# The blocks of a feed-forward product redrawn, and stored partial rows added in DRAM and by VectorE instead of on the way back into SBUF

## The chip, the cores and the metric

The kernel runs on one core of a Trainium2 chip. TensorE (PE) multiplies, VectorE (DVE) and ScalarE (ACT) work on tiles in SBUF and PSUM, GpSimd (POOL) and SyncE (SP) issue DMAs. The metric is the device time of one execution in microseconds (us); the time shown for a kernel is the median of its runs.

## The reference

One layer of a diffusion backbone over 512 latent tokens of width 1024, with 256 context tokens ahead of them. The token mixer (a pooling branch and a bidirectional mLSTM) comes first; the change lies in the feed-forward part behind it:

```python
x = x + g1 * mix_lat
x = x + g2 * _swiglu(_modulate(x, norm_ffn[l], sh2, sc2), w_ffn_in[l], w_ffn_out[l])
...
return _rmsnorm(x, norm_final)

def _swiglu(h, w_in, w_out):
    g, u = jnp.split(h @ w_in, 2, axis=-1)
    return (jax.nn.silu(g) * u) @ w_out
```

The hidden width is 2816, that is 22 tiles of 128. All values are float32.

## The kernel before

Everything is kept transposed: features on the 128 partitions, the 512 tokens along the free dimension. A float32 operand is split into a rounded high part (a cast by ScalarE, `wh`, `oh`, `gh`) and the remainder (a subtraction by VectorE, `wl`, `ol`, `gl`), and each product is made of three TensorE matmuls: high by high, high by low, low by high (`mm3`). So every weight tile that is loaded costs one cast and one subtraction before TensorE can use it.

**First product.** For each hidden tile `j` the gate and the up product form a 2 by 2 block matrix (gate and up by the two halves of the tokens and of the 1024 input features), and a `Pair` computes it with seven block products instead of eight (Strassen and Winograd's scheme). `prepare` loads the pair's two weight rows, one into `wr` and one into `ur` (512 KB each, by SP), forms the sums S1 to S4 of their blocks on VectorE, and splits all of them. For blocks named in `sent` the low part is made by a DMA that adds the weight from DRAM onto the negated high part (`ol`, issued by POOL, L1036). `front` runs the products A11, S1, S2 and A12, `back` runs S3, S4 and A22. After S3, VectorE adds bank and copy (`third`, L1124); A22 is added onto the same bank, so TensorE waits for that addition. `done` splits the finished hidden tile into `act`.

**Second product.** The 22 hidden tiles are worked off in blocks, each block multiplied with its part of `w_ffn_out` and added onto the residual:

- a *plain first block* (hidden tiles 0 to 3 before the change): for each of the 8 output rows one sum over the block's tiles with 512 tokens per matmul (`ffn_out`), which VectorE scales by `g2` and adds onto the residual `x1` in SBUF (L1415). Each finished row is stored to a DRAM buffer `x1d`;
- *two blocks of six tiles* (4 to 9 and 10 to 15): the block's hidden tiles are kept as block operands and their sums (`Even`, `Odd`), and four `Out` items compute two output rows each with seven block products. Their results, scaled by `g2`, go to two DRAM buffers `od` (8 rows each, 256 KB a row) by DMAs on POOL;
- a *plain last block* (16 to 21): `x1` is loaded back from `x1d`, both `od` buffers are added onto it by DMAs that accumulate into SBUF (L1477, 16 of them on POOL), and `ffn_out` runs over the two token halves separately, since the final norm of the first half is computed beside the products of the second.

`run` walks over a list of items and interleaves the back of one item with the front of the next; `made(after)` issues the next item's whole preparation one item ahead, and `also(it)` is called after each item and holds the loads of `x1`. Where TensorE passes from the last `Odd` of a block to the first `Out` (`joint`), the whole back of the `Odd` comes ahead of two steps of the item after.

Instructions of one engine are put in order by a scheduler, as far as `issue_after` and data dependencies leave it free; SP and POOL issue their DMAs in that order and stop at the first one whose buffer or source is not ready. `wr` has three buffers, `ur` two. PSUM has four `ps` banks and four `pat` banks; the plain sums take three of the `ps` banks in turn. At the very end `dense(8)` and `dense(9)` issue matmuls whose result nobody reads, around the last sums of squares.

## Time and profile before

| | before |
|---|---|
| median of 3 runs | 897.86 us |
| lowest of 3 runs | 897.61 us |
| the profiled execution's own time | 899.67 us |
| its span in the profile | 897.9 us |
| mean granted TensorE clock | 0.993 |
| TensorE matmul busy | 874.6 us, 97% of the span |
| VectorE busy | 652.8 us, 73% |
| ScalarE busy | 470.7 us, 52% |
| GpSimd busy | 98.1 us, 11% |
| mean DMA rate | 150 GB/s |

Times in the profile are counted from the start of the span. "L1124" is a line of the kernel before; in the changed kernel the lines up to about 1130 stand one further down. In a wait, the arrow points at the instruction that ended it. "PEclk" is the granted clock of TensorE, 1.00 being full speed. The feed-forward part that the change touches begins at about 525 us.

### The profile page before, as it was taken

To read this page: it belongs to the slowest core of one execution; us is meant where nothing else is said; L and a number is where in the kernel's file an instruction comes from. 1 tells how busy PE (TensorE), PEld (TensorE's weight loads), DVE (VectorE), ACT (ScalarE), POOL (GpSimd) and SP (SyncE) were. 2 spreads that over 40 slices of the span, in tenths; PEclk is the share of its full clock that TensorE was granted. 3 is DMA by queue.
4 is the path that set the end of the run, shared out by engine and by line. 5 is a ranking of instruction groups with operands and counts; after the bars stand their busy time and mean duration, and the time that the engine had idled before them with its cause. 6 is when DMAs were issued, how large, how long until landed. Compare 5 with 4: busy or idle time off the path is not lost.

```text
span 897.9 us, 15849 instructions
## 1 busy us (share of the span) xinstructions
PE 874.6 (97%) x6112; PEld 805.4 (90%) x6112; DVE 652.8 (73%) x1292; ACT 470.7 (52%) x919; POOL 98.1 (11%) x137
## 2 busy tenths in 40 slices
PE   9999999999999999999999999999999999998896
PEld 8689798899889998889988899879999999998896
DVE  4678677768876788667886659578888788856544
ACT  4454453545445453354545456446757775755442
POOL 0000000110000100001000000031202220221510
PEclk9999999999999999999999999999999999998999
DMA  9863021445352642526354710379637863794862
GB/s 350 317 201 99 25 71 60 164 129 153 106 177 66 194 112 76 191 69 199 98 153 154 276 48 25 94 211 239 142 103 218 218 147 99 223 283 103 181 127 95
DMA packets 48557, 134.59 MB, mean 150 GB/s; under 512 B 5440, under 2 KB 9824, under 8 KB 47456
## 3 DMA queue, kind: packets, MB, share of 16 engines
q1 hardware_dynamic: 38208, 112.06, 39.0%
q0 software_dynamic: 10272, 21.50, 11.7%
q8 instruction: 48, 0.79, 0.3%
q14 instruction: 29, 0.24, 0.1%
HBM read 123.56 MB, written 9.98 MB: 149 GB/s over the span
## 4 chain that ended last, share of the span: by engine, by line
PE 85%; DVE 6%; DMA 3%; ACT 3%; issue 2%; DVEq 0%; SPq 0%; ACTq 0%
PE ps L188 10%; PE ps L189 10%; PE ps L190 10%; PE ps L198 8%; PE ps L195 8%; PE ps L196 8%; PE pat L348 3%; PE ps L579 3%; PE ps L580 3%; PE ps L581 3%; PE pat L189 2%; PE pat L188 2%; PE pat L190 2%; PE pat L793 2%; PE pat L795 2%
## 5 line engine op out<-in xcount | busy, mean ns | idle before, releaser
L195 PE MATMUL ps<-a,wh 128*128 128x512 f32 x272 | 106.5, 392 | 0.0
L196 PE MATMUL ps<-a,wh 128*128 128x512 f32 x272 | 106.3, 391 | 0.0
L158 ACT CAST wh<-wr 128x1024 fp32r<-128x1024 f32 (+3 forms) x69 | 66.7, 969 | 63.4 <-PE ps L196 34.8
L159 DVE TENSOR_TENSOR wl<-wr,wh 128x1024 fp32r<-128x1024 f32 (+3 forms) x69 | 78.2, 1133 | 28.7 <-ACT wh L158 17.5
L198 PE MATMUL ps<-a,wl 128*128 128x512 f32 x272 | 68.0, 391 | 0.0
L196 PEld LDWEIGHTS ps<-a,wh 128*128 128x128 f32 x272 | 51.1, 188 | 10.2
L198 PEld LDWEIGHTS ps<-a,wl 128*128 128x128 f32 x272 | 50.9, 188 | 10.4
L195 PEld LDWEIGHTS ps<-a,wh 128*128 128x128 f32 x272 | 51.1, 188 | 10.1
L188 PE MATMUL ps<-hp,oh 128*128 128x256 f32 x176 | 50.8, 289 | 8.7 <-DVE tmp L1124 8.1
L1036 POOL DMA_DIRECT2D ol<-in_wffi x42 | 37.1, 882 | 146.6 <-ACT ol L1035 61.5
L188 PE MATMUL ps<-hp,gh 128*128 128x256 f32 x176 | 49.8, 283 | 2.9 <-ACT pat L1086 2.9
L190 PE MATMUL ps<-hp,ol 128*128 128x256 f32 x176 | 50.3, 286 | 0.0
L189 PE MATMUL ps<-hp,oh 128*128 128x256 f32 x176 | 50.2, 285 | 0.0
L189 PE MATMUL ps<-hp,gh 128*128 128x256 f32 x176 | 49.0, 278 | 0.0
L190 PE MATMUL ps<-hp,gl 128*128 128x256 f32 x176 | 48.9, 278 | 0.0
L177 ACT CAST gh<-sg 128x1024 fp32r<-128x1024 f32 (+1 forms) x27 | 26.7, 989 | 41.5 <-DVE sg L1050 26.5
L538 DVE SCALAR_TENSOR_TENSOR pb<-pb,crow_s 128x1024 f32<-128x1024 f32 x32 | 39.1, 1239 | 11.9 <-DMA pb<-in_wada_b 11.8
L188 PEld LDWEIGHTS ps<-hp,oh 128*128 128x128 f32 x176 | 34.6, 197 | 9.4 <-DVE tmp L1124 8.5
L793 PE MATMUL pat<-vh,Sp 128*128 128x258 f32 x144 | 41.1, 285 | 0.0
L794 PE MATMUL pat<-vl,Sp 128*128 128x258 f32 x144 | 40.7, 283 | 0.0
L795 PE MATMUL pat<-vh,Sp 128*128 128x258 f32 x144 | 40.7, 282 | 0.0
L178 DVE TENSOR_TENSOR gl<-sg,gh 128x1024 fp32r<-128x1024 f32 (+1 forms) x27 | 30.9, 1145 | 11.6 <-ACT gh L177 11.6
(422 smaller groups left out, 3031.2 us busy)
## 6 DMA issues: line engine op xcount, KB each, us to landing
wr<-in_w SPq DMA_DIRECT2D x42, 512.0 KB, 3.6
pb<-in_wada_b SPq DMA_DIRECT2D x32, 512.0 KB, 4.3
wr<-in_wffi SPq DMA_DIRECT2D x25, 512.0 KB, 4.8
ol<-in_wffi POOLq DMA_DIRECT2D x42, 256.0 KB, 5.8
ur<-in_wffi SPq DMA_DIRECT2D x19, 512.0 KB, 4.2
ada<-in_wada_a SPq DMA_DIRECT2D x8, 1024.0 KB, 9.9
wr<-in_wffo SPq DMA_DIRECT2D x16, 384.0 KB, 5.2
wr<-in_wout SPq DMA_DIRECT2D x8, 512.0 KB, 3.7
```

The source lines that it names most:

```text
L158: nc.scalar.copy(wh, raw[:, :n])
L159: V.tensor_sub(wl, raw[:, :n], wh.bitcast(F32))
L188: nc.tensor.matmul(dst, wh, ah, start=first and i == 0, stop=False, skip_group_check=on)
L189: nc.tensor.matmul(dst, wh, al, start=False, stop=False, skip_group_check=on)
L190: nc.tensor.matmul(dst, wl, ah, start=False, stop=last and i == n - 1, skip_group_check=on)
L195: nc.tensor.matmul(dst, wh, ah, start=first and i == 0, stop=False)
L196: nc.tensor.matmul(dst, wh, al, start=False, stop=False)
L198: nc.tensor.matmul(dst, wl, ah, start=False, stop=last and i == len(wparts) - 1)
L538: V.scalar_tensor_tensor(wa[:, :D], wa[:, :D], 0.5, crow_s, ALU.mult, ALU.mult, accum_out=mods[:, i:i + 1])
L793: nc.tensor.matmul(o, sh_, vh[:, s, :], start=n == 0, stop=False)
L794: nc.tensor.matmul(o, sh_, vl[:, s, :], start=False, stop=False)
L795: nc.tensor.matmul(o, sl_, vh[:, s, :], start=False, stop=n == len(srcs) - 1)
```

## The change

The blocks are redrawn: the plain first block takes hidden tiles 0 to 4 (five instead of four), the two blocks of seven products take 5 to 10 and 11 to 16, the plain last block takes 17 to 21 (five instead of six). The number of pairs stays 22 and the number of `Out` items stays 8.

- The first block now runs its two pairs (tiles 3 and 4) through `run`, and then the eight output rows; before, three of the output rows were interleaved with the back of the one pair.
- The first six rows of `x1` are stored by POOL as before, the last two by SP, after the preparation of the first item of the second block.
- The first `od` buffer is added onto `x1d` in DRAM, one row per pair, by DMAs on POOL: during the six pairs of the second block of six and two of the last pairs. Each is ordered after the second `ol` DMA of the following item.
- The rows of `x1` are loaded back after the last pair's `ur` load instead of two per pair during the last pairs. In `prepare`, `loaded` now names the `ur` load.
- The second `od` buffer is loaded into SBUF by SP (six buffers for the eight rows) and added by eight VectorE additions, ordered after the last hidden tile's split.
- At `joint` the three steps of the `Odd`'s back now alternate with the steps of the `Out`'s front.

```diff
-        nc.sync.dma_start(b, wb)
-        p["loaded"] = nc.sync.dma_start(a, wa)
+        p["loaded"] = nc.sync.dma_start(b, wb)
+        nc.sync.dma_start(a, wa)
...
-            split(self.s, *self.dst)
+            nc.scalar.copy(self.dst[0], self.s)
+            self.over = V.tensor_sub(self.dst[1], self.s, self.dst[0].bitcast(F32))
...
             joint = isinstance(it, Out) and not isinstance(prev, Out)
+            if joint:
+                next(b)
             if not it.begun:
                 next(f)
+                if joint:
+                    next(b)
                 next(f)
             if joint:
-                for _ in b:
-                    pass
+                next(b)
...
-    od = {c0: dram.tile([KT, P, T], F32, name=f"od{c0}") for c0 in (4, 10)}
+    od = {c0: dram.tile([KT, P, T], F32, name=f"od{c0}") for c0 in (5, 11)}
...
+    starts = (5, 11)
+    turn = itertools.count(NP + 1)
+    plain = [third] + [Pair(j, next(turn)) for j in range(NP + 1, starts[0])]
+    for _ in run(plain).back():
         pass
-    b = third.back()
-    next(b)
-    next(b)
-    wf, af = [], [ffn_bank(), ffn_bank(), banks[3]]
-    for j, acc in enumerate(af):
-        if j == 2:
-            next(b)
-        wf.append(wchunk(j, 0, c1, raw=None if j else tl("ur", [P, D], F32, 2)))
-        mm3_low_last(acc, wf[j][:NP], act[:NP], last=False)
-    for j, acc in enumerate(af):
-        mm3(acc, wf[j][NP:], act[NP:c1], first=False)
-        ffn_out(j, ALL, None, 0, c1, acc)
-        nc.gpsimd.dma_start(x1d[j], x1[j])
-    for j in range(3, KT):
+    turn_[0] = plain[-1].turn % 3
+    c1 = starts[0]
+    for j in range(KT):
         ffn_out(j, ALL, wchunk(j, 0, c1), 0, c1)
-        nc.gpsimd.dma_start(x1d[j], x1[j])
+        if j < KT - 2:
+            nc.gpsimd.dma_start(x1d[j], x1[j])
...
+    for j in (KT - 2, KT - 1):
+        nc.sync.dma_start(x1d[j], x1[j])
...
+    rows = iter([(c, j) for c in starts[:-1] for j in range(KT)])
...
+            bufs["act"] = 2 * (c1 - c0)
             x1[:] = [S("x1") for _ in range(KT)]
-        elif it in plain:
-            with tc.issue_after(plain[min(plain.index(it) + 1, len(plain) - 1)].p["loaded"].ins):
-                for j in itertools.islice(back_, 2):
+        if it in ins[6:] + plain[1:-1]:
+            after = items[items.index(it) + 1].p.get("added")
+            with tc.issue_after(after.ins) if after else ExitStack():
+                for c, j in itertools.islice(rows, 1):
+                    nc.gpsimd.dma_start(x1d[j], od[c][j], accum_op=ALU.add, max_dma_last_dim=2048)
+        if it is plain[-2]:
+            with tc.issue_after(plain[-1].p["loaded"].ins):
+                for j in range(KT):
                     nc.sync.dma_start(x1[j], x1d[j])
-        if it is plain[-2]:
-            with tc.issue_after(plain[-1].p["added"].ins):
-                for j in range(KT):
-                    for c in (4, 10):
-                        nc.gpsimd.dma_start(x1[j], od[c][j], accum_op=ALU.add)
...
+    def added(j):
+        o = tl("od", [P, T], F32, 6, LINE)
+        with tc.issue_after(plain[-1].p["loaded"].ins):
+            nc.sync.dma_start(o, od[starts[-1]][j])
+        with tc.issue_after(plain[-1].over.ins):
+            V.tensor_add(x1[j], x1[j], o)
+
+    for j in range(KT):
+        added(j)
```

How the change moves instructions is seen at two places.

The first is SP's queue of loads at the beginning of the plain last block. `wr` and `ur` are the two weight rows of a pair, `x_1491` and following are the rows of `x1`. Before:

```order
L1018 DMA ur_9137<-in_wffi 128x1024
L1019 DMA wr_9400<-in_wffi 128x1024
L1018 DMA ur_9269<-in_wffi 128x1024
L1472 DMA x_1491_9128<-x1d 128x512
...
L1472 DMA x_1496_9133<-x1d 128x512
L1019 DMA wr_9532<-in_wffi 128x1024
L1472 DMA x_1497_9134<-x1d 128x512
L1472 DMA x_1498_9135<-x1d 128x512
L1018 DMA ur_9401<-in_wffi 128x1024
```

After, where `wr_9558` and `ur_9559` belong to the very last pair, and `od_9838` is the first row of the second `od` buffer on its way to SBUF:

```order
L1020 DMA wr_9558<-in_wffi 128x1024
L1019 DMA ur_9428<-in_wffi 128x1024
L156 DMA wr_9869<-in_wffo 128x640
L1019 DMA ur_9559<-in_wffi 128x1024
L1479 DMA x_1509_9288<-x1d 128x512
...
L1479 DMA x_1515_9294<-x1d 128x512
L1487 DMA od_9838<-od_5503 128x512
...
L1487 DMA od_9853<-od_5503 128x512
L156 DMA wr_9875<-in_wffo 128x640
L156 DMA wr_9881<-in_wffo 128x640
L1479 DMA x_1516_9295<-x1d 128x512
```

Before, two more pairs' `ur` loads stand behind the rows of `x1` in the queue; after, every pair's loads stand ahead of them, and seven rows of `x1` and six of `od` follow in one piece. The last row of `x1` comes two weight loads later, and the last two rows of `od` (not shown) at the end, once two of the six `od` buffers have been read.

The second place is VectorE right behind the last hidden tile's split (`act`), up to the first sums of the plain last block. Before:

```order
L1129 SCALAR_TENSOR_TENSOR tmp_9761<-tmp_9705,tmp_9761 128x256
L1133 SCALAR_TENSOR_TENSOR tmp_9761<-ps_6276,tmp_9761 128x256
L178 TENSOR_TENSOR act_9779<-tmp_9761,act_9778 128x512
L1415 SCALAR_TENSOR_TENSOR x_1491_9128<-ps_6274,lb,x_1491_9128 128x256
L1415 SCALAR_TENSOR_TENSOR x_1492_9129<-ps_6275,lb,x_1492_9129 128x256
```

After, with the eight additions of the rows of `od`:

```order
L1134 SCALAR_TENSOR_TENSOR tmp_9777<-ps_6276,tmp_9777 128x256
L1139 TENSOR_TENSOR act_9795<-tmp_9777,act_9794 128x512
L1489 TENSOR_TENSOR x_1509_9288<-x_1509_9288,od_9838 128x512
L1489 TENSOR_TENSOR x_1510_9289<-x_1510_9289,od_9841 128x512
...
L1489 TENSOR_TENSOR x_1516_9295<-x_1516_9295,od_9859 128x512
L1420 SCALAR_TENSOR_TENSOR x_1509_9288<-ps_6274,lb,x_1509_9288 128x256
L1420 SCALAR_TENSOR_TENSOR x_1510_9289<-ps_6275,lb,x_1510_9289 128x256
```

All eight additions stand in one piece between the last split and the first instruction that reads a bank of the plain last block (L1415, now L1420). At the same place TensorE's order has changed: the 17 matmuls of `dense` stand behind the third sum of the last block,

```order
L190 MATMUL ps_6276<-act_9795,gh_9883 128x256
L191 MATMUL ps_6276<-act_9794,gl_9884 128x256
L1508 MATMUL ps_6277<-hp_5497 128x256 x17
L189 MATMUL ps_6274<-act_9355,gh_9889 128x256
L190 MATMUL ps_6274<-act_9356,gh_9889 128x256
```

where `ps_6276` is the third bank and `ps_6274` the first bank in its second use, while before they stood at the kernel's end:

```order
L190 MATMUL ps_6274<-act_9778,wl_9882 128x256
L1497 MATMUL ps_6277<-hp_5497 128x256 x8
L238 MATMUL pat_6280<-ones,tmp_9922 128x2 x2
L1497 MATMUL ps_6277<-hp_5497 128x256
L238 MATMUL pat_6280<-ones,tmp_10257 128x2 x2
L1497 MATMUL ps_6277<-hp_5497 128x256 x8
```

The scheduler, which orders these matmuls freely, has moved all 17 from the end to the place where TensorE needs the first bank back.

More of the change, by code (lines that the diff above doesn't have):

```diff
@@ L58, in layer_kernel @@
     shifted = {"ac"}
+    bufs = dict(BUFS)
     def open_pool(name, tags, side="left"):
@@ L432, in queries @@
         return [conv_part(lat_tile(Q0 + 2 * h + dk), T, 2 * h + dk,
-                          [tl("q", [P, T + NEXT], F32R, BUFS["q"], LINE)[:, NEXT:] for _ in range(2)]) for dk in range(2)]
+                          [tl("q", [P, T + NEXT], F32R, bufs["q"], LINE)[:, NEXT:] for _ in range(2)]) for dk in range(2)]
     def keys(h):
@@ L1422, in wchunk @@
         return wload(wffo[j][:, c0 * P:c1 * P], (c1 - c0) * P, dst, skip, raw)[0]
[L1427 to L1451 removed]
+    starts = (5, 11)
+    turn = itertools.count(NP + 1)
+    plain = [third] + [Pair(j, next(turn)) for j in range(NP + 1, starts[0])]
+    for _ in run(plain).back():
+        pass
+    turn_[0] = plain[-1].turn % 3
+    c1 = starts[0]
+    for j in range(KT):
+        ffn_out(j, ALL, wchunk(j, 0, c1), 0, c1)
+        if j < KT - 2:
+            nc.gpsimd.dma_start(x1d[j], x1[j])
+    items, ins = [], []
+    for c0 in starts:
         evens = []
@@ L1455, in layer_kernel @@
             evens.append(Even(j, t, j == c0 + 4, evens[0].turn if evens else t))
-            items += [evens[-1], Odd(j + 1, next(turn), evens[-1])]
+            ins += [evens[-1], Odd(j + 1, next(turn), evens[-1])]
+            items += ins[-2:]
         items += [Out(j, next(turn), evens, c0, c0 + 6) for j in range(KT // 2)]
-    c0, c1 = 16, FT
+    c0, c1 = starts[-1] + 6, FT
     plain = [Pair(j, next(turn)) for j in range(c0, c1)]
-    back_ = iter(range(KT))
+    items += plain
+    made(items[0])
+    for j in (KT - 2, KT - 1):
+        nc.sync.dma_start(x1d[j], x1[j])
+    close_pool("late4")
+    close_pool("late0")
+    open_pool("late0", ("bo", "nf", "ev"))
+    rows = iter([(c, j) for c in starts[:-1] for j in range(KT)])
     def also(it):
@@ L1464, in also @@
             close_pool("late0")
-            open_pool("late0", ("act", "before_act", "x1"))
+            open_pool("late0", ("act", "before_act", "x1", "od"))
             tl("before_act", [P, NEXT], F32, 1, LINE)
             shifted.add("act")
+            bufs["act"] = 2 * (c1 - c0)
             x1[:] = [S("x1") for _ in range(KT)]
-        elif it in plain:
-            with tc.issue_after(plain[min(plain.index(it) + 1, len(plain) - 1)].p["loaded"].ins):
-                for j in itertools.islice(back_, 2):
-                    nc.sync.dma_start(x1[j], x1d[j])
-        if it is plain[-2]:
-            with tc.issue_after(plain[-1].p["added"].ins):
-                for j in range(KT):
-                    for c in (4, 10):
-                        nc.gpsimd.dma_start(x1[j], od[c][j], accum_op=ALU.add)
-    made(items[0])
-    for _ in run(items + plain, also=also).back():
-        pass
+        if it in ins[6:] + plain[1:-1]:
[6 more added lines that the diff above has]
+                for j in range(KT):
+                    nc.sync.dma_start(x1[j], x1d[j])
+    for _ in run(items, also=also).back():
+        pass
+    def added(j):
[6 more added lines that the diff above has]
+        added(j)
     SumSq.banks = banks[4:]
```

10 lines of the change are left out of this document (1 added, 9 removed).

## The prediction

> **What bounds the kernel now.** I read the page first: which engine is full.
>
> ```profile
> PE 874.6 (97%) x6112; PEld 805.4 (90%) x6112; DVE 652.8 (73%) x1292; ACT 470.7 (52%) x919; POOL 98.1 (11%) x137
> ```
>
> TensorE is busy for all but about 23 us, so an edit that takes no matmul away can only win back idle time, and the slow clock behind it. The second view is TensorE's waits, over the feed-forward part from 560 us on (total, times, longest).
>
> ```profile
> PE ps L188 <- DVE tmp L1124: 8.1, 2, 4.8
> PE ps L188 <- ACT pat L1086: 2.9, 4, 1.6
> PE ps L188 <- ACT bo L177: 1.2, 2, 0.6
> PE ps L188 <- ACT act L177: 1.2, 1, 1.2
> ```
>
> The first line is more than half of it: two waits, 4.8 and 3.3 us long. In the view by windows I looked for them and for what the clock did; the columns are length, busy time and starts of PE, of weight loads, DVE, ACT and POOL, then the granted clock, DMA share and GB/s.
>
> ```profile
> 604.00:608.00 4.00, 2.69 (x24) 2.49 (x22) 3.74 (x5) 3.05 (x5) 1.03 (x2) 1.00 1.06 271
> ...
> 808.00:812.00 4.00, 0.00 (x0) 0.00 (x0) 1.70 (x4) 0.23 (x1) 0.00 (x0) 0.69 0.35 100
> 812.00:816.00 4.00, 3.92 (x18) 3.93 (x19) 3.51 (x6) 3.87 (x7) 0.62 (x1) 0.50 0.00 0
> ...
> 848.00:852.00 4.00, 1.41 (x6) 1.41 (x7) 3.09 (x7) 3.38 (x7) 3.55 (x4) 0.81 1.12 234
> 852.00:856.00 4.00, 4.00 (x30) 4.00 (x29) 2.15 (x4) 0.62 (x1) 0.81 (x1) 0.77 1.11 232
> ...
> 870.00:880.00 10.00, 10.00 (x90) 10.00 (x89) 4.67 (x11) 4.10 (x10) 0.00 (x0) 1.00 0.01 2
> ```
>
> The last row gives the normal pace of a 128x256 matmul: 10.00/90 = 0.111 us. Behind the first gap the clock is 0.50 and 18 matmuls start where 36 would fit: 18 x 0.111 = 2.0 us more. Behind the second, 36 starts take 5.4 us instead of 4.0: 1.4 us more. So gap A costs 4.8 + 2.0 = 6.8 us, gap B 3.3 + 1.4 = 4.7 us. The chain of waits says what each waited for (start, length, what).
>
> ```profile
> 799.35 10.83 DMA ur<-in_wffi
> 810.27 0.70 DVE sg L1049
> 811.61 0.43 DVE tmp L1124
> ...
> 842.21 6.03 DMA wr<-in_wffo
> 848.26 0.63 ACT oh L171
> 848.91 0.69 DVE ol L172
> 849.60 0.45 DVE act L178
> 850.12 0.43 DVE tmp L1124
> ```
>
> In both, VectorE stood at the first instruction on a weight row that had not landed, and L1124, which TensorE needed, was queued behind it. Who held the two loads up stands in the rows of the lines that load and accumulate `x1`, each with its DMAs' time to landing (minimum, median, maximum), and of `ur`:
>
> ```profile
> L1472 SPq DMA_DIRECT2D x<-x1d x8: 381/416/797, 790.8 to 796.1; - x8
> DMA to landing us min/median/max: 4.7/8.8/12.2
> ...
> L1018 SPq DMA_DIRECT2D ur<-in_wffi x18: 327/328/333, 572.2 to 815.1; - x18
> DMA to landing us min/median/max: 3.0/4.0/10.8
> ...
> L1477 POOL DMA_DIRECT2D x<-od x16: 873/1060/2296, 836.3 to 861.5; - x16
> DMA to landing us min/median/max: 4.7/6.8/11.7
> ```
>
> A: eight rows of `x1` (2 MB) were issued from 790.8 to 796.1, just ahead of the `ur` load of 799.35, which took 10.83 us where the median is 4.0. B: the 16 accumulating DMAs ran from 836.3 to 861.5, over the weight load of 842.21.
>
> **The change part by part.** *Gap A.* No row of `x1` now stands ahead of a pair's load; only single accumulating DMAs fall there. At 4.0 us the load lands 6.8 us earlier, which covers the wait of 4.8. I take off all of A, -6.8 (ends -5.0 if 1.8 of it returns, and -6.8). Late next is the `x1` and `od` traffic behind the last `ur` load, which only the last block's weights share.
>
> *Gap B.* The 16 accumulations are gone from this place; the order of the steps is not: weight split, load, cast, split, `act`, L1124. What stays open is how fast the load lands.
>
> ```profile
> wr<-in_wffo SPq DMA_DIRECT2D x3, 384.0 KB, 4.4
> ...
> wr<-in_wffo SPq DMA_DIRECT2D x5, 256.0 KB, 3.4
> ```
>
> These are the medians of such loads from 817 to 836 and from 565 to 600. The load is now 320 KB, between the two: 3.9 us, 2.1 less than 6.03. Of 3.3 us of idle 1.2 stay; a second small split (128 columns) now comes ahead of `act`, 0.2 more. 1.4 us of idle stay, and I expect the clock to hold, since the window from 604 to 608, with 1.3 us of idle, shows it at 1.00. B: -4.7 + 1.4 = -3.3 (ends -4.7, and 0 if the load still takes 6.03).
>
> *The eight additions.* VectorE does them between the last split and the first L1415. Rows for the pace of such an operation, and for the end of the last pair before:
>
> ```profile
> 817.00 0.69 DVE L1057 TENSOR_TENSOR sg<-sg,wr 128x512 f32<-128x512 f32 x1
> 817.60 0.69 DVE L178 TENSOR_TENSOR act<-tmp,act 128x512 fp32r<-128x512 f32 x1
> ...
> 853.56 0.42 DVE L1133 SCALAR_TENSOR_TENSOR tmp<-ps,tmp 128x256 f32<-128x256 f32 x1 [0.52 <-PE ps L190]
> 854.67 0.69 DVE L178 TENSOR_TENSOR act<-tmp,act 128x512 fp32r<-128x512 f32 x1 [0.69 <-ACT act L177]
> 857.54 0.88 DVE L1415 SCALAR_TENSOR_TENSOR x<-ps,lb,x 128x256 f32<-128x256 f32 x2 [2.17 <-PE ps L190]
> ```
>
> One starts 0.60 us after the other. On the times of before: TensorE ends the pair at 853.5. It then has 24 matmuls on four finished tiles (2.7), 6 on the fifth (0.7) and the third sum of 15 (1.7), and at 858.6 needs the first bank again. VectorE ends the last split at 855.4, the additions at 855.4 + 8 x 0.60 = 860.2, and half of the row of two L1415 (0.88) frees the bank at 860.6. The seventh row of `od` can only be asked for once the first addition has freed its buffer, at 856.0; with 3.4 us (the 256 KB weight load above) it lands at 859.4 where VectorE would want it at 859.0: 0.4 more. So TensorE gets the bank at 861.0, 2.4 us late. The 17 `dense` matmuls (17 x 0.111 = 1.9 us) lie in that wait; 0.5 us stays idle, and the clock should hold. Term: +2.4. Ends: +1.9, what `dense` alone takes there, and +8.8, if the last `od` rows land after the median 8.8 us of the crowded `x1` loads (the eighth, asked for at 856.6, at 865.4; addition 0.6 and L1415 0.44 to 866.4, plus 1.0 of slow clock, half of A's share).
>
> *The end of the kernel.* One `dense` matmul stood between the two last sums of squares:
>
> ```profile
> 888.68 0.22 PE ps L1497
> ```
>
> That goes, -0.2; the runs of eight on either side lay beside ScalarE's square and POOL's power.
>
> *The first block.* The wait for `act` (1.2 us, the last line of the waits) had two matmuls of cover too few per row; now twelve of 512 columns lie ahead of it, so it goes. But the second pair must now be split where VectorE and ScalarE are still at work on the first, and its A11 may wait for its casts. No row shows that; the nearest are the waits for L1086, 0.7 us on average and 1.6 at most. I take 1.2, so 0 in all (ends -1.2 and +2.0). The next pairs' weights get 0.6 us more per output row (15 matmuls instead of 12, at the pace below), which should shorten the L1086 waits at the following transition: -0.5 (ends -1.6 and 0).
>
> *The alternation at the first `Out`.* The two waits for `bo`, the block operands that the `Out` products read, lie there. S3's 12 matmuls (1.3 us) now lie ahead of the first `Out` product: -1.0 (ends -1.2 and 0).
>
> *The tile that moves* from the last block to the first is worked in 24 matmuls of 512 columns instead of 48 of 256.
>
> ```profile
> 592.00:596.00 4.00, 4.00 (x19) 3.31 (x18) 1.35 (x2) 0.62 (x1) 0.54 (x1) 1.00 0.79 256
> ```
>
> A 512-column matmul takes 4.00/19 = 0.21 us: 48 x 0.111 - 24 x 0.21 = 0.3 us, -0.3. The number of seven-product steps is the same.
>
> *The eight accumulations in DRAM.* No row of before shows one. The nearest is the burst into SBUF, whose queue in the window from 838 to 856 read:
>
> ```profile
> q0 software_dynamic: 1558, 2.85, 92.4%
> ```
>
> 2.85 MB, 11 rows of 256 KB, took 92.4% of 16 engines for 18 us: 1.5 us of all engines a row. It is ordered behind the second `ol` DMA of a pair. Gap A shows the slack: 6.8 us late made a wait of 4.8, so 2.0 us are free. 1.5 lies below that. I take +0.8 for the whole (0.1 a row), ends 0 and +12 (8 x 1.5). The Trainium skill, "DMA: Bandwidth & Descriptors", section "Issuing engines are not separate DMA queues", speaks against this part: DMAs issued from ScalarE, SyncE or GpSimd run on the same 16 engines and interleave. Gap A agrees, with 10.83 us against 4.0. By that rule alone, with no slack, this term would be +12 instead of +0.8.
>
> Sum: -6.8 - 3.3 + 2.4 - 0.2 + 0 - 0.5 - 1.0 - 0.3 + 0.8 = -8.9. The profiled execution took 899.67 us (span 897.9), so 890.8 of the same kind; the median of the runs lies 1.8 lower at 897.86, which gives 889.0.
>
> **The rivals.** *Late rows at the end.* The loads of `x1` must wait for the accumulation of their row, and SP stops at the first that cannot go: the seventh and eighth rows' accumulations are issued during the last pairs, and weight loads stand behind both. For: the accumulations into SBUF took up to 11.7 us. Against: they were 16 at once; the minimum is 4.7. Then B keeps its 4.7 and the additions rise by up to 6.4: between 892.3 and 898.7, say 895.5.
>
> *The wait is moved, not removed.* 3.3 MB of `x1` and `od` rows still have to come in within some 30 us, now behind the last `ur` load; the weight row that follows on SP comes late, VectorE stands at its split, and A returns one pair later, with its clock: 889.0 + 6.8 = 895.8. For: the split stands ahead of L1124 in the order. Against: 3.3 MB at the 232 GB/s of the quoted window from 852 to 856 are 14 us.
>
> *Accumulations take the loads' time*: each of the eight costs its pair the 1.5 us, with no slack: 889.0 - 0.8 + 12 = 900.2, within the 2% of no change. Against it: the slack of 2.0 us.
>
> *Slower: the low halves come late.* The `ol` loads share POOL's queue with the accumulations, and one stands right behind each.
>
> ```profile
> 825.36 0.87 POOL L1036 DMA_DIRECT2D ol<-in_wffi  x1 [6.00 <-ACT tmp L1121]
> 828.10 0.87 POOL L1036 DMA_DIRECT2D ol<-in_wffi  x1 [1.87 <-ACT pat L1086]
> ...
> 841.85 0.28 PE L190 MATMUL pat<-hp,ol 128*128 128x256 f32 x1
> ...
> DMA to landing us min/median/max: 3.9/5.8/11.0
> ```
>
> An accumulation would go out at 825.4 + 0.9 = 826.3; the `ol` load issued at 828.1 is needed at 841.85 and takes 5.8 (the last row is L1036's). If it had to wait for the accumulation to land, TensorE stands still from the point at which that takes over 841.85 - 5.8 - 826.3 = 9.8 us. At 13 us, a little over the longest seen, each of the eight costs 3.2 and some 1.4 of slow clock: 8 x 4.6 = 37, giving 925. Against: a single one is nearer to the minimum of 4.7.
>
> *More is won*: the ends on the good side (B whole, first block -1.2, transition -1.6) give about 885.
>
> **How the numbers follow.** Forecast 0.60; late rows 0.14; wait moved 0.10; loads' time 0.06; low halves late 0.04; more won 0.06. The likeliest, 889.0, is the predicted time. From 885 to 896 lie the forecast with its ends, most of "more won", and the first two rivals but for their worst: about 8 in 10; the other two lie above. By over 2% (18 us, about what a measurement of this kernel tells from no change) faster would need nearly all idle time of the kernel gone: 0.02. Slower by over 2%: the low halves late and a little for what I have not seen, 0.05. Within: 0.93.
>
> **What would show it.** In the profile after: no wait for L1124 of over 2 us and a granted clock of 1.00 from 560 us to the last sums; `ur` loads within 6 us; one idle time of TensorE of about half a microsecond behind `dense`, ended by the first L1420; VectorE's eight additions within 5.5 us. Wrong would be: a gap of over 3 us anywhere in the last pairs, additions that wait for `od`, SP held at a row of `x1` while a weight row is due, or matmuls that wait for `ol`.

## The result

The kernel after took 902.27 us (median of 5 runs, 900.06 to 902.96) against 897.61 us for the kernel before beside it. The ratio is 1.0052, with an interval of 1.0031 to 1.0074: 0.5% slower, and not 1% faster as forecast (889.0 us, range 885 to 896). Run twice more, each time beside the kernel before on one chip, it came out at 1.0012 (0.9998 to 1.0026) and 1.0018 (1.0002 to 1.0034). So by the three ratios the loss is between 1 and 5 us, nearer to 1 or 2 in the two larger samples, and the gain is not there. The profiled execution took 900.06 us, the least of its five, with a span of 898.3 us against 897.9 before (899.67 us, above its median), and a mean granted clock of 0.992 against 0.993; so the two profiles show 0.4 us of the difference and account for where the forecast gain went. They do not show why the median lies 2.2 us above the profiled execution. TensorE's busy time, from the page of the kernel after, is what it was (874.6 us before):

```profile
PE 874.0 (97%) x6088; PEld 803.4 (89%) x6088; DVE 657.9 (73%) x1300; ACT 471.5 (52%) x919; POOL 88.7 (10%) x127
```

So the idle time has only changed its place. TensorE's waits of the kernel after from 560 us on (total, times, longest):

```profile
PE ps L189 <- ACT pat L1087: 9.3, 9, 5.7
PE pat L191 <- DMA ol<-in_wffi: 1.4, 1, 1.4
PE ps L191 <- DMA ol<-in_wffi: 1.2, 1, 1.2
PE pat L255 <- POOL rc L247: 1.1, 1, 1.1
...
PE ps L189 <- DVE tmp L1125: 0.4, 1, 0.4
```

The line that led before, 8.1 us in two waits for L1124 (L1125 now), has shrunk to 0.4. In its place stands one wait of 5.7 us for a copy by ScalarE, L1087; TensorE's waits for that copy were 0.7 us on average before. The windows around it (columns as in the prediction) show no matmul for a whole window, and the clock at 0.50 behind it:

```profile
836.00:840.00 4.00, 2.89 (x25) 2.68 (x24) 0.00 (x0) 0.00 (x0) 0.00 (x0) 1.00 0.73 282
840.00:844.00 4.00, 0.00 (x0) 0.00 (x0) 2.72 (x4) 3.58 (x7) 0.67 (x1) 0.81 0.31 77
844.00:848.00 4.00, 3.38 (x16) 3.38 (x17) 1.37 (x3) 1.49 (x4) 0.21 (x1) 0.50 0.46 71
848.00:852.00 4.00, 4.00 (x31) 4.00 (x31) 2.08 (x4) 1.50 (x4) 0.00 (x0) 0.84 0.30 82
```

From 844.6 to 852, 47 matmuls start where 7.4/0.111 = 66 would fit, so some 2 us are lost on top of the 5.7. The chain of waits of the kernel after through that place (start, length, what), and SP's timeline with the instructions that it issued, say why:

```profile
816.86 8.65 DMA x1d<-od
...
825.52 4.48 DMA x<-x1d
...
830.07 9.89 DMA wr<-in_wffo
...
842.89 0.42 DVE tmp L1130
843.31 0.34 DVE tmp L1134
...
844.20 0.37 ACT pat L1087
```

```profile
816.43 9.41 SPq L1479 DMA_DIRECT2D x<-x1d  x7
825.93 2.96 SPq L1487 DMA_DIRECT2D od<-od  x6
829.19 1.22 SPq L156 DMA_DIRECT2D wr<-in_wffo  x2
```

The timelines of ScalarE and VectorE show the split of that load; the brackets give how long the engine had stood idle, and what ended it:

```profile
840.05 0.72 ACT L178 CAST gh<-wr 128x640 fp32r<-128x640 f32 x1 [11.42 <-DMA wr<-in_wffo]
840.80 0.82 DVE L179 TENSOR_TENSOR gl<-wr,gh 128x640 fp32r<-128x640 f32 x1 [9.60 <-ACT gh L178]
```

The third weight row of the last block was asked for at 830.07, behind 13 rows of `x1` and `od` on SP, and took 9.89 us to land; SP itself had stood before the seventh row of `x1` until that row's accumulation landed. ScalarE and VectorE reach the split of that weight row (L178, L179) some 10 us before it can start, and behind that split stand L1130, L1134 and the copy L1087 for which TensorE waits. It is gap A again, with other rows ahead of another load, in a later pair; it is called the new gap below. It is no accident of one execution: in the traces of the two repetitions the wait is 6.2 and 5.6 us long.

The eight additions came as forecast. VectorE's timeline of the kernel after:

```profile
858.86 4.90 DVE L1489 TENSOR_TENSOR x<-x,od 128x512 f32<-128x512 f32 x8
863.68 1.26 DVE L1420 SCALAR_TENSOR_TENSOR x<-ps,lb,x 128x256 f32<-128x256 f32 x3
```

They follow each other without a wait for an `od` row, and TensorE stands still for 0.4 us behind the `dense` matmuls (its wait for L1420).

For the account, the span is cut at instructions that both kernels have: the end of the plain first block's last addition onto `x1`, the second, tenth and sixteenth store of an `Out` result, the end of the last `act`, the first addition onto `x1` with 256 columns. Times in us, from the timelines of VectorE and POOL. "Work moved" is what the table of blocks moves: a pair is 84 matmuls of 256 columns (84 x 0.111 = 9.3), a tile is 24 x 0.21 = 5.0 in the first block and 48 x 0.111 = 5.3 in the last.

| stretch | before | after | work moved | difference left | forecast |
|---|---|---|---|---|---|
| to the end of the first block | 603.3 | 617.9 | +14.3 | +0.3 | 0 |
| to the second store (transition, new turn) | 73.8 | 72.7 | | -1.1 | -1.5 |
| to the tenth store (four `Out`, the six pairs of the second block) | 89.4 | 92.3 | | +2.9 | +0.8 |
| to the sixteenth store (four `Out`) | 24.8 | 25.1 | | +0.3 | |
| last pairs | 64.0 | 50.9 | -9.3 | -3.8 | -10.1 |
| additions | 2.2 | 4.7 | | +2.5 | +2.4 |
| to the end | 40.4 | 34.6 | -5.3 | -0.5 | -0.2 |
| the tile's wider matmuls | | | | -0.3 | -0.3 |
| sum | 897.9 | 898.3 | | +0.4 (+0.3 by the rounded rows) | -8.9 |

Two rows carry the miss: the last pairs, 6.3 us, and the pairs of the second block, 2.1 us. Every other row is within 0.4 us of its forecast.

### The profile page after: what moved, and what is told of

Its sections match the earlier page's. It is cut to its first block, busy times and chain, and to the rows that moved or that the text cites. A ratio compares the mean times of both kernels' runs of the same rounds, so it can differ in the third digit from the quotient of the medians.

```text
span 898.3 us, 15806 instructions
## 1 busy us (share of the span) xinstructions
PE 874.0 (97%) x6088; PEld 803.4 (89%) x6088; DVE 657.9 (73%) x1300; ACT 471.5 (52%) x919; POOL 88.7 (10%) x127
## 4 chain that ended last, share of the span: by engine, by line
PE 72%; issue 8%; DMA 8%; DVE 6%; ACT 4%; POOL 1%; DVEq 0%; POOLq 0%; SPq 0%; ACTq 0%
PE ps L189 8%; PE ps L190 8%; PE ps L199 8%; PE ps L191 8%; PE ps L197 7%; PE ps L196 7%; DMA ur<-in_wffi 3%; PE pat L349 3%; PE ps L580 3%; PE ps L581 3%; PE ps L582 3%; PE pat L794 2%; PE pat L795 2%; PE pat L796 2%; DMA wr<-in_wffo 1%
## 5 line engine op out<-in xcount | busy, mean ns | idle before, releaser
L189 PE MATMUL ps<-hp,gh 128*128 128x256 f32 x176 | 50.9, 289 | 9.4 <-ACT pat L1087 9.3
L189 PE MATMUL ps<-hp,oh 128*128 128x256 f32 x176 | 49.2, 280 | 1.0 <-ACT oh L1032 0.5
L190 PE MATMUL ps<-hp,oh 128*128 128x256 f32 x176 | 48.8, 277 | 0.0
L178 ACT CAST gh<-sg 128x1024 fp32r<-128x1024 f32 (+1 forms) x27 | 26.7, 988 | 39.5 <-DVE sg L1051 30.3
L189 PEld LDWEIGHTS ps<-hp,gh 128*128 128x128 f32 x176 | 33.6, 191 | 11.6 <-ACT pat L1087 11.5
L179 DVE TENSOR_TENSOR gl<-sg,gh 128x1024 fp32r<-128x1024 f32 (+1 forms) x27 | 30.9, 1145 | 11.0 <-ACT gh L178 11.0
```

The lines of the kernel that those rows point to most:

```text
L189: nc.tensor.matmul(dst, wh, ah, start=first and i == 0, stop=False, skip_group_check=on)
L190: nc.tensor.matmul(dst, wh, al, start=False, stop=False, skip_group_check=on)
```

## The experiments

All were run beside the kernel before on one chip; the table has each median, that of the kernel before beside it, and the ratio with its 95% interval. Kernels with the same time of before ran together on one chip; what ran again as a base for its group is in italics. The edits are shown shortened.

| run | us | before | ratio |
|---|---|---|---|
| weight rows first | 898.47 | 899.73 | 0.9988 (0.9976 to 1.0001) |
| dense at the end | 900.61 | 899.73 | 1.0015 (1.0003 to 1.0028) |
| no sums in DRAM | 896.31 | 899.73 | 0.9965 (0.9949 to 0.9981) |
| old turn | 902.33 | 899.73 | 1.0032 (1.0020 to 1.0044) |
| *after, again* | 900.92 | 900.28 | 1.0012 (0.9998 to 1.0026) |
| two rows late | 899.71 | 900.28 | 0.9999 (0.9984 to 1.0014) |
| stores add | 892.49 | 900.28 | 0.9919 (0.9895 to 0.9942) |
| split later | 898.22 | 900.28 | 0.9971 (0.9953 to 0.9989) |
| *stores add, again* | 892.29 | 898.83 | 0.9932 (0.9916 to 0.9948) |
| before, rows late | 892.88 | 898.83 | 0.9927 (0.9909 to 0.9946) |
| first store adds | 898.65 | 898.83 | 1.0000 (0.9987 to 1.0013) |
| before, stores add | 893.01 | 898.83 | 0.9940 (0.9926 to 0.9954) |
| *before, rows late, again* | 892.07 | 898.80 | 0.9913 (0.9889 to 0.9938) |
| after, sums as before | 890.36 | 898.80 | 0.9898 (0.9872 to 0.9923) |
| *after, a third time* | 900.49 | 898.80 | 1.0018 (1.0002 to 1.0034) |
| *after, sums as before, again* | 892.73 | 899.47 | 0.9916 (0.9898 to 0.9935) |
| fifth split later | 890.55 | 899.47 | 0.9895 (0.9876 to 0.9913) |

The theory at the outset: the gain of gap A was taken off, but the wait had moved to the next load that stands behind bulk rows on SP; beside it the accumulations in DRAM cost more than the 0.8 us put down. The rival: the loss lies in the second block and at the end of the kernel alone.

### The weight rows first

```
-    with issue_after(last ur load): load x1[0..7], od rows
+    with issue_after(last ur load): load x1[0..5]
+    weight rows 1, 2, 3 of the last block
+    with issue_after(weight row 3): load x1[6], x1[7], od rows
```

> The kernel after, with one thing moved on SP's queue: the second and third weight rows of the last block are asked for behind the sixth row of x1, ahead of the two rows of x1 that wait for the last accumulations and of the od rows. Theory (the wait was moved, not removed): TensorE's idle time of 5.7 us for L1087 at 838.9 and the 2.0 us of slow clock behind it go, 902.3 - 7.7 = 894.6, and the eight additions still take about 4.9 us in one piece. Rival 1 (it moves once more): the od rows, asked for later, come late to the additions, one to four of which then wait for them; 5 to 7 us come back in front of the first L1420 and the time stays at 900 to 902. Rival 2 (the gap is not where the time went; the accumulations and the end of the kernel are): the gap goes, but under 3 us are won, 899 or more.

Measured 898.47 us: the gap for L1087 is gone, the additions are in one piece, and still only part is won. In its own trace (its lines stand one further down) TensorE's waits and the chain have

```profile
PE ps L190 <- DVE tmp L1126: 5.4, 2, 3.9
```

```profile
836.74 7.27 DMA wr<-in_wffo
844.09 0.73 ACT gh L179
844.85 0.83 DVE gl L180
...
845.70 2.84 DMA wr<-in_wffo
848.56 0.63 ACT oh L173
...
850.62 0.43 DVE tmp L1126
```

The fourth weight row now stands behind the two `x1` rows and the six `od` rows and lands at 844.0. The fifth is asked for when the fourth's split is done (845.70), lands at 848.5, and L1126 stands behind its split: 3.9 us of idle time, and then 1.7 us of slow clock between 852 and 856. The first rival had the right idea (it moves once more) but named the wrong place, the additions. The bulk rows hit whichever weight row comes next.

### Dense at the end

```
-    dense(8); sd = rstd_cols(...); dense(9)
+    with issue_after(last product): dense(8)
+    sd = rstd_cols(...)
+    with issue_after(last sum of squares): dense(9)
```

> The kernel after, with the 17 dense matmuls held behind the last product, eight ahead of the last sums of squares and nine behind them, where the kernel before had them. Theory A (their absence at the end let the clock fall to 0.50 and 0.62 over the last sums and the L255 rows; they covered nothing that matters at the additions): 1.0 to 2.2 us less, 900.1 to 901.3, with a granted clock of 0.9 or more over the last 8 us; TensorE then stands idle for 2.3 us ahead of the first L1420. Theory B (as on record: at the end they lay beside waits and cost or bring nothing; beside the additions they keep the clock up): no change at the end, and the idle time of 2.3 us at the additions brings up to 1 us of slow clock: 902.3 to 903.3.

Measured 1.0015 of before, where the kernel after has 1.0012 to 1.0052: no difference that these runs can tell. The 17 matmuls cover nothing but the idle time that the additions make, as the prediction had it; without them TensorE waits, in this kernel's waits and windows,

```profile
PE ps L190 <- DVE x L1421: 2.4, 1, 2.4
```

```profile
868.00:870.00 2.00, 2.00 (x19) 2.00 (x19) 1.31 (x5) 1.95 (x6) 0.00 (x0) 1.00 0.00 0
```

and the clock stays at 1.00 behind it. At the end of the kernel they are worth 0.5 us at most (34.1 us to the end against 34.6).

### Without the sums in DRAM

```
-        if it in ins[6:] + plain[1:-1]: ... dma_start(x1d[j], od[c][j], accum_op=add)
```

> The kernel after without the eight accumulating DMAs into x1d: the first stored block of six tiles is left out of the sum. Theory A (the accumulations cost far more than the 0.8 us put down for them, in the second block, where the span between the first and the last stored row grew by 4.4 us, and at the end, where the seventh row held SP for 5 us): 3 to 4.5 us come back in the second block and at least 3 us of the 7.7 at the gap for L1087, so 894 to 896. Theory B (0.8 us, and the gap comes from the 3.3 MB themselves, whoever holds SP): 900 to 901.5, with the gap for L1087 still over 4 us. If both hold by half (second block back, gap kept): 898.

This kernel leaves the first stored block out of the sum. Measured 896.31 us, 0.9965 of before, just above theory A's 894 to 896. SP is not held by an accumulation any more, yet most of the new gap stays; this kernel's waits have

```profile
PE ps L189 <- ACT pat L1087: 8.3, 7, 3.7
```

So 2.0 us of the 5.7 came from SP's stand and the accumulations beside it, and 3.7 stay with the rows alone: each theory holds for a part. The six pairs of the second block (eighth to tenth store) took 66.3 us here. Over the kernels, one trace each: with accumulations in DRAM 67.4, 69.2, 67.1 (after, three times), 68.2, 69.2, 67.7, 68.8 and 66.6, mean 68.0; without them, in kernels with the new table of blocks and plain stores, 66.3, 65.4, 65.2 and 65.5, mean 65.6; in the kernel before 64.6. So the accumulations cost 2.4 us there in the mean, with no overlap between the two groups, and up to 1 us comes in with the rest of the change (64.7 and 65.0 in two further traces with the old blocks).

### The old turn into Out

```
-            if joint: next(b)        # back of the pair, in three steps between the fronts
+            if joint: for _ in b: pass
```

> The kernel after with the turn into the first Out of each block as it was: the last step of the pair ahead of it is run to its end behind the first two Out products, not between them. Theory (as on record: the new turn wins 1.0 us, once per block at most): 903.3 to 904.3, with waits for bo of about 1.2 us in all. Rival (the new turn is part of the loss, as TensorE works on the pair's last products while the blocks wait): 900 to 901.5.

Measured 1.0032 of before; the kernel after lies between 1.0012 and 1.0052, so the median settles nothing. The trace has the waits for the block operands back that the prediction spoke of,

```profile
PE ps L189 <- ACT bo L178: 1.2, 2, 0.6
```

and the second block's four `Out` took 26.0 us against 25.1 in all three runs of after. But another kernel with the new turn, the fifth split later, took 26.0 us there too. A gain of up to 1 us from the new turn fits, and is not shown.

### Two rows late

```
-    load x1[0..7] ; od rows ; weight rows 2, 3, 4
+    load x1[0..5] ; od rows ; weight rows 2, 3, 4 ; load x1[6], x1[7]
```

> The kernel after with only the two rows of x1 moved that wait for the last accumulations: on SP's queue they come behind the fourth weight row of the last block; six od rows stay ahead of the second. Theory (what made the weight row late is that SP stood for 5.7 us at the seventh row of x1, and what was then asked for in one bunch): the second and third weight rows land by 833, the fourth by 841, and neither the gap for L1087 (7.7 us with its clock) nor the one for L1126 that came in its place when the od rows were moved too (3.9 us and 1.7 of clock) is there: 902.3 - 7.7 = 894.6, or 0.992 of before. Rival (the twelve rows that still stand ahead are enough to make it late): 3 to 5 us of the gap stay, 898 to 900.

Measured 899.71 us, 1.2 us under after, with a gap of 5.4 us still there. Here the theory failed in one point: not holding SP is not enough. SP's timeline and the chain:

```profile
821.70 8.67 SPq L1488 DMA_DIRECT2D od<-od  x6
830.63 13.17 SPq L157 DMA_DIRECT2D wr<-in_wffo  x3
```

```profile
821.15 10.03 DMA x<-x1d
831.25 10.53 DMA wr<-in_wffo
```

SP did not wait for an accumulation now, but for rows of `x1` to land before it issued the last three `od` rows and the weight rows, the third of which was so asked for at 831.25. Twelve rows are 3.1 MB; at the 251 GB/s that all transfers together moved between 816 and 840 they take 12.5 us, and the weight row behind them lands at 841.8, as late as ever. So no accumulation has to hold SP for the row to be late: the bytes ahead of a load with a date are enough.

### The split later

```
-    wl_ = [wchunk(j) for j in range(8)]
+    wl_ = [wchunk(j) for j in range(2)]
+    with issue_after(third of the last pairs: its act): wl_.append(wchunk(2))
+    wl_ += [wchunk(j) for j in range(3, 8)]
```

> The kernel after with no transfer moved: only the split of the third weight row (cast on ScalarE, subtraction on VectorE) is held until the third of the last five pairs has its act, some eight instructions later on either engine. Theory (the late row costs time because its split stands in order ahead of what TensorE needs): the row lands as late as before, about 840, but the idle time for L1087 falls from 5.7 to about 2.4 us, and the clock holds or falls for less: 902.3 - 3.3 - up to 2.0 = 897 to 899. Rival (TensorE waits for the traffic in another way, through the low halves or its own weights): the idle time stays over 5 us and the time at 901 to 903.

No transfer is moved here, only the order in which ScalarE and VectorE take up the late row. Measured 898.22 us, 2.7 us under after in its group. The waits between 834 and 852 (this kernel's L1091 is L1087, its L1129 is L1125) are

```profile
PE ps L193 <- DVE tmp L1129: 2.2, 1, 2.2
PE ps L193 <- ACT pat L1091: 1.9, 1, 1.9
```

The 5.7 us shrink to 1.9 with the row as late as before, and 2.2 us come back at the fifth row, which is asked for only when the fourth's split is done, with a slow clock from 852 to 856. So the time is lost because the engines take their work in order, and a late operand stops everything queued behind it. The theory held in size and place.

### The kernel before with its rows late

```
-        elif it in plain: (two rows of x1 behind each pair's loads)
+        if it is plain[-2]: with issue_after(last ur load): load x1[0..7]
```

> The kernel before with one thing moved: its eight loads of x1 stand on SP's queue behind the last ur load, not around it. Its 16 accumulating DMAs into x1 stay. Theory (eight rows can be hidden behind the last ur load, sixteen with the weight rows cannot): the gap of 4.8 us and its 2.0 us of slow clock go and do not come back one pair later; the second gap (3.3 + 1.4) stays, as the 16 accumulations still lie over the weight load: 0.992 to 0.993 of before. Rival (a gap is always moved to the next weight row): an idle time of 3 us or more for L1086 or L1124 comes between 830 and 842, and the time is 0.997 to 1.000 of before.

This is the kernel before with one thing moved, and it measured 892.88 and 892.07 us, 6 and 6.7 us under the kernel before. TensorE's waits of its first run, where of the two gaps only a part of gap B is left (2.3 us here, 3.1 in the second run):

```profile
PE ps L188 <- ACT pat L1086: 3.0, 5, 1.6
PE ps L188 <- DVE tmp L1124: 2.3, 1, 2.3
```

Gap A is gone and did not come back one pair later: eight rows (2 MB) behind the last `ur` load make no gap, and twelve or more, in the kernels above, do. The term of -6.8 in the prediction is right for this edit.

### Stores that add

```
-            nc.gpsimd.dma_start(od[c0][2 * j], o)
+            nc.gpsimd.dma_start(x1d[2 * j], o, accum_op=ALU.add)
-    accumulations into x1d, od loads, eight additions
```

> The kernel after with each Out product's store adding its two tiles straight into x1d, for both stored blocks: the 16 stores into od become 16 accumulating stores, and the eight accumulations between DRAM tiles, the eight loads of od and VectorE's eight additions go. Theory: the 2.6 us at the additions, 1.2 to 3.0 us in the second block, and the 7.7 us of the gap go, since SP is no longer held and eight rows less are on the queue: 902.3 - 11.5 to 13.3 = 889 to 891, or 0.986 to 0.988 of before. Rival 1 (an accumulating store moves each byte twice and takes POOL longer, so the low halves behind it on POOL come late): 16 times 0.3 to 0.6 us of that come back, 894 to 900. Rival 2 (the last two stores land late and SP stands at the seventh row of x1 as it did): the gap of 7.7 stays, 897 to 899.

Measured 892.49 us, 8.4 us under after, and 892.29 in a second run. With eight rows only on SP, no idle time over 1.4 us is left in the waits:

```profile
PE ps L189 <- ACT pat L1087: 6.1, 11, 1.4
```

The first rival holds in part. The first of an `Out`'s two stores, accumulating, holds POOL for 0.87 us, not 0.56, and lands in a median of 4.2 us, not 2.4 (the second: 6.4, not 5.2); four `Out` with such stores took 24.8 to 27.0 us, 26.3 in the mean (second to eighth store and tenth to sixteenth, over four runs), against 24.8 in the kernel before and 24.1 to 26.0 in all runs with plain stores.

> The kernel before, with its blocks of 4, 6, 6 and 6 tiles and its own turn into Out, in which each Out store adds straight into x1d, the 16 accumulations into x1 go, and the eight loads of x1 stand behind the last ur load. Theory (the gain lies in the rows that no longer come in over the weight loads, and the rest of the change, five tiles first and last and the new turn, brings the 1.1 us between the first block and the first store and the 0.4 us at the end): both gaps go, and it comes out 1 to 2 us over the kernel of this group whose Out stores add: 0.993 to 0.995 of before. Rival (the rest of the change is a loss, which the stores hide): 2 us or more under it, 0.988 to 0.990.

The same stores in the kernel before, with its rows late, gave 893.01 us, 0.7 us over the kernel of its group with the new blocks. The rival, 2 us or more under it, did not come; the 0.7 us itself is not clear of the noise.

```
+            if first stored block: dma_start(x1d[j], o, accum_op=ALU.add)
+            else: dma_start(od[j], o)
-    accumulations into x1d
```

> The kernel after with the first stored block's Out stores adding into x1d; the second stored block is stored, loaded and added by VectorE as in after. Theory (two costs, one in the second block from the accumulations between DRAM tiles, one at the end from sixteen rows ahead of a weight row): the six pairs of the second block take 65 to 66.5 us, not 67 to 69; the gap for L1087 stays at 3 to 5 us, as where the accumulations were left out; the additions keep their 2.6 us: 5 us under after, 0.995 to 0.997 of before. Rival (only the rows that SP stood at made the gap): the gap falls under 1.5 us, 0.991 to 0.993.

Measured 898.65 us, 1.0000 of before, and the theory missed half: the additions and the gap at L1087 (3.4 us, not under 1.5 as the rival had it) came as expected, but the six pairs took 68.5 us without any accumulation among them. One wait of 2.0 us with a slow clock behind it is in that stretch, in its waits from 734 to 744 and the window behind:

```profile
PE ps L189 <- ACT pat L1087: 2.0, 1, 2.0
```

```profile
742.00:744.00 2.00, 2.00 (x12) 2.00 (x11) 1.72 (x4) 0.00 (x0) 0.54 (x1) 0.54 0.74 195
```

Take off its 2.0 and the 1.7 of clock, and 64.8 is left. Why that wait came here stays open. It also says that the 2.4 us above hold in the mean and not for each trace: two rows late, with its 68.8 us, has such a wait of 2.1 us with a slow clock as well.

### The kernel after with the sums as before

```
-    accumulations into x1d, od loads, eight additions by VectorE
+    for j in range(8): for c in starts:
+        nc.gpsimd.dma_start(x1[j], od[c][j], accum_op=ALU.add)     # during the last pairs, as before
```

> The kernel after (blocks of 5, 6, 6 and 5 tiles, new turn into Out) with the stored rows added as before, by 16 accumulating DMAs into x1 during the last pairs; its eight loads of x1 stand behind the last ur load already. Theory A (the partition and the turn bring what was put down for them, about 1.1 us between the first block and the first store and 0.4 us at the end, and all of the loss is in the new way of adding): 1 to 2 us under the kernel before with its rows moved, 0.991 to 0.992 of before, six pairs of the second block in 64.5 to 66 us. Theory B (part of the loss comes with the partition or the turn: the pairs of the second block stay at 66 us or more without any accumulation there, as where these were left out): 0.5 to 2 us over it, 0.994 to 0.996.

Measured 890.36 us beside 900.49 for after and 892.07 for the kernel before with its rows late; in a second run 892.73. So the new way of adding costs 10.1 us, all of the loss and more, and the new blocks and turn with the old way of adding lie 1.7 us under the old blocks in the one comparison on one chip (the ratios of the four runs, 0.9898 and 0.9916 against 0.9913 and 0.9927, say about 0.13%, with overlapping intervals). Theory A's 1 to 2 us and its six pairs (65.4 and 65.2 us) came, and theory B's loss did not; but whether the new blocks win anything the intervals leave open. What is left is gap B, in a smaller form in this trace (4.2 us in the second run's):

```profile
PE ps L189 <- DVE tmp L1125: 3.2, 1, 3.2
```

> The same kernel with the split of the fifth weight row held on ScalarE behind the fourth of the last five pairs' act cast and on VectorE behind the last pair's L1125 (L1128 in its own numbering); no transfer is moved. Theory (the place of the split in the order): the idle time of 3.2 us and the slow clock of 1.7 us go, and at most 1 us comes back where the next splits follow: 4 to 5 us under the base, 885.5 to 886.5. Rival (the accumulations make the row late for whoever needs it next): the wait turns up at the last pair's act or at the first sums, and under 1.5 us are won.

```
+    held = fourth of the last pairs: its act cast, last pair: its L1125
     wl_.append(wchunk(4))     # cast and subtraction behind these
```

Measured 890.55 us beside 892.73, 0.9895 of before. The wait for L1125 is gone, the clock stays at 1.00, and 0.2 to 1.2 us come back at four places, 2.2 us together; the trace gains 3.4 us of span, the median 2.2, between the theory's 4 to 5 and the rival's 1.5. Both kernels are faster than before and than after: the later rows were worth keeping, the additions were not, and the partition and the turn at least cost nothing.

## Why the prediction was wrong

**What bounds it, and the two gaps:** right. The place, size and cause of both were read rightly; the kernel before with its rows late won 6 to 6.7 us against -6.8 on record.

**The step that failed** is in the paragraph on gap A: "I take off all of A" with "late next is the `x1` and `od` traffic behind the last `ur` load, which only the last block's weights share". What is late next was named and costed at nothing. It was then made a rival ("the wait is moved, not removed") with 0.10, and its description is what happened: VectorE at its split, a weight row late on SP, the clock lost too (the instruction kept waiting was the copy L1087, not L1124). It cost 5.7 + 2.0 us against the 6.8 put down. The argument against it, 14 us of transfer within some 30 us, set the bytes against the whole stretch and not against the first date in it. By the same figures: 13 rows are 3.4 MB, 14.7 us at 232 GB/s; begun at 816.4 they end at 831.1, and the two weight rows of 320 KB behind them at 833.9. In the kernel after TensorE ran dry at 838.9 and went on 4.7 us after the row had landed, so the row was due at 834.2. The sum leaves 0.3 us of slack, where the prediction set 14 us against some 30, and no room for SP's stand or for POOL's transfers, with which the row came at 840.0. A chance of 0.10 was far too low for that; how high it should have been, the rows quoted ahead of the run do not settle, since the date itself comes from the trace after.

The Trainium skill, "DMA: Bandwidth & Descriptors", section "Issuing engines are not separate DMA queues", has DMAs of all issuing engines interleave on the same 16 engines. The trace of the kernel after agrees: POOL's `ol` loads asked for while SP's rows came in (816 to 830) took 6.4 to 8.1 us to land, the one asked for at 843.3 took 4.1. Gap A, which the prediction gives as agreeing, does not test this, since its rows and its late load were both issued by SP.

What the prediction left out is SP's own queue, where the rows stand ahead: in the kernel after, SP's 17 loads from 816.0 to 833.7 landed in the order in which they were asked for, the third weight row (839.97) behind the last of the six `od` rows (838.34).

**Gap B:** 0.4 us of idle time where 1.4 were expected, which was at least in part luck: behind the new gap the row had more time. Where the new gap was taken away or cut while the rows stayed, 2.2 to 3.9 us came back at L1125 (the split later, the weight rows first). The two gaps together, -10.1 on record, measured -3.8.

**The accumulations in DRAM** were mis-sized: +0.8 on record, 2.4 us measured in the second block, and 2.0 of the 5.7 us at SP. The issue on POOL (862, 1186 and 1200 ns) and the landing are in the group of their line:

```profile
L1475 POOL DMA_DIRECT2D x1d<-od x8: 862/1186/1200, 711.7 to 825.8; - x8
...
DMA to landing us min/median/max: 4.4/7.6/8.8
```

The slack of 2.0 us that was to cover them was read from a late load on SP in the last pairs. In the second block POOL stood 3.3 us before the first accumulation until the sixth `od` store had landed (711.20), and the `ol` loads behind the accumulations landed 1.6 to 4.7 us later than in the kernel without them. The +12 that the prediction works out with no slack was further off, on the other side.

**The additions** (+2.4, measured +2.5) and **the end** (-0.2, -0.5) were right; only the 0.4 us for a late `od` row did not come. **The first block** (0, +0.3) was right in the sum and in part by luck: the wait for `act` went as forecast, but of the 1.9 us that came in its place only 0.5 are a wait for a cast (L1032), and 1.4 are the wait for an `ol` load in the list above, which the prediction did not name. **Transition and turn** (-1.5, -1.1): the waits for the copy fell from 2.3 to 1.9 us and that for `bo` from 0.6 to 0.3, and a wait of 0.6 us for the first block's last addition (L1415), at the boundary of the two stretches, is gone, which the prediction did not name. With the old way of adding the new blocks and turn came out 1.7 us better, where -1.8 had been put down for transition, turn and tile; that is not clear of the noise.

**Late rows at the end** was right in that SP stood at the seventh row (5.7 us), wrong in that the additions would wait: they ran in one piece. Three of the four signs of being wrong that the prediction names came: a gap of over 3 us in the last pairs, SP held at a row of `x1`, and matmuls that wait for `ol`. **Accumulations take the loads' time** and **low halves late** did not come at their prices; TensorE's waits for `ol` are 1.2 us in the second block and 1.4 in the first. **The range** was too narrow because two rivals could hold at once: the 6.3 us of the one and the 2.1 us of the other make 8.4 of the 9.3 us between the forecast and the profile, and the range held each alone.

## What to carry to other kernels

Bulk loads that are moved off one load with a date land in front of the next one: for every load behind them ask when its first user stands in line, and set bytes ahead of it against the time up to that date, not against the whole stretch. An engine that works in order stops at the first operand that is late, so a split placed a few instructions later can be worth as much as a load that comes earlier. Of a change with several parts, run each part alone: here the later rows by themselves won 6 to 7 us, and the new way of adding beside them cost 10.

## What the runs showed of the hardware

The clock did not follow the length of a gap alone. It fell to 0.54 behind an idle time of 2.0 us (first store adds, 740 to 742) and to 0.57 behind 2.2 us (the split later), and stayed at 1.00 behind 2.4 us (dense at the end, 865 to 868) and 2.3 us (before, rows late); every gap of 3.1 us or more was followed by a slow stretch. The place of the gap decides. In the clock's record of each trace the slow stretches between 560 and 880 us are 3.41 or 6.83 us long and begin and end on one grid of 3.41 us (before: 809.49, 816.32, 850.45, 853.86). Over the 19 traces and that stretch the clock, where it was full, fell at the end of each grid step in which TensorE had stood idle for 2.04 us or more in all, and of none with 1.83 us or less; no step lay between. The gap of 2.3 us (838.75 to 841.05) was cut by the grid at 839.25 and left 1.8 us in one step. So whether a gap of 2 to 3 us costs a slow stretch, some 1.7 us, is a matter of where it falls. The Trainium skill, "TensorE: Matmul & The Clock Gate", Part 1, puts the fall after a whole idle window of 3.4 us that runs free of the program; the grid agrees with the length, but the 2.0 us here are shorter than such a window, so in these traces less than a whole one was enough.

A DMA that accumulates from one DRAM tile into another, 256 KB, took 4.4 to 8.8 us to land in the kernel after, and one from SBUF into DRAM 3.9 us at least, where the plain store of before took 2.3 at least; POOL was held 1.19 and 0.87 us for the issue instead of 0.56. And SP, with nine rows of 256 KB asked for in 5.2 us, issued each further load only when the one eight places ahead of it had landed (two rows late: the fourth `od` row at 826.17, the second `x1` row in at 826.11; the third weight row at 831.25, the sixth `x1` row in at 831.18). An instruction that waits for a semaphore stands ahead of these loads on SP; whether anything but the program sets this limit, no run here shows.
